# The last four v tiles of a PEER layer, multiplied bank by bank behind the fold of the gathered sums

## Chip, cores and metric

One core of a Trainium2 chip. The metric is the device time of one execution in microseconds; the kernel before took a median of 940.72 us (3 runs, 939.09 to 942.44).

## What is computed

A decoder block for 256 tokens of width 1024. Two attention mixers (MoBA and NSA) and their merge come first; what the change touches is the last part, the PEER expert layer, and the output:

```python
def peer_ffn(h, w_q, sub_k1, sub_k2, expert_u, expert_v):
    ...
    def per_chunk(args):
        xc, ec, gc = args
        u = expert_u[ec]
        a = jnp.einsum('cd,chkd->chk', xc, u).astype(jnp.float32)
        w = (jax.nn.gelu(a) * gc).astype(xc.dtype)
        return jnp.einsum('chk,chkd->cd', w, expert_v[ec])
```

There are 16384 experts (`expert_u` and `expert_v` are 16384 x 1024 float32, 64 MB each). Each token uses 8 heads x 16 experts. The block returns `x + peer_ffn(rmsnorm(x))`.

## The kernel before, in words

The expert layer splits the 256 tokens. For 160 of them (`ND`) the layer is done densely, over all experts: 128 u tiles of 128 experts are loaded (512 KB each) and multiplied with the normed tokens (`u_tile`, L588), Gelu and gate give `ga`, and then 128 v tiles are loaded and multiplied with `ga` (L850 to L858). For the other 96 tokens (`NG`) only the chosen experts' rows are gathered: 96 steps gather 128 u rows each (512 KB) and dot them with the token (L622), 96 steps gather 128 v rows each and add them, weighted, to the sums `accG` on VectorE (L631 and L633).

**The v loop** (L850). For tile `i` eight matmuls, one for each 128 columns of the model width, accumulate over all 128 tiles in four PSUM banks, `acc[0]` to `acc[3]`, two column blocks of 160 tokens each. Then VectorE copies one column of the tile to `mark` (L857), and `gather_steps` issues gather steps, 0.9 a tile (`STEPS_V`), each placed behind the mark on VectorE; from tile 124 on it issues all that are still open. The tiles are loaded on SP's queue (`load_raw`, L580) into nine buffers (three tags of three); tile `i + 9` is loaded when tile `i` has been read by its matmuls and its mark. A gather step (`gathers`, L602) works on rows that POOL fetched by an indirect DMA (L611); there are four row buffers in two pairs, and after every odd step `n` POOL fetches rows `n + 3` and `n + 4`.

**The gathered sums.** `accG` has two sets of 1024 columns (for tokens in groups of 64 and of 32); each set's 128 partitions hold partial sums of several slots of the same token. The steps go through the 64-set and the 32-set of each half of the heads, so the last sixteen steps add to the second set alone. A matmul with the constant matrix `fold` (L865) sums the partials and puts them on the partitions of tokens 0 to 95.

**The end** (L859 to L876). `accT` gets the four banks as copies, two by VectorE, two by ScalarE (L868); its first 96 token columns are cleared on POOL (L860). The result stands as columns by tokens, so it is turned: four PSUM banks `fin`, one for each half of the tokens (`h`) and half of the columns (`j`), take first the folded sums (`h` = 0 only) and then, as matmuls with an identity (L872), the blocks of `accT`. VectorE adds the residual in `x1` (L875), and SP writes 256 KB (L876). This is done four times, one bank after the other.

On each engine the instructions run in a fixed order. It is made when the program is built: in the order of the source, except that work which the builder takes for ready passes work which it takes for late.

Of the kernel before, what the change touches and what calls it, by code (L numbers as in the profile page):

```python
# [18 lines left out]
P = 128  # L19
S = 256  # L20
NH = 2
# [7 lines left out]
NKEY = 128  # L29
# [8 lines left out]
NG = sum(SETS)  # L38
ND = S - NG
STEPS_R = 0.55  # L40
STEPS_U = 0.8
STEPS_V = 0.9
GT = 4
HEAT = 9
AHEAD = 1
# [25 lines left out]
def block_kernel(ctx: ExitStack, tc, x, g2, consts, small, wqkv, wkv5, wmg, w1kv, wup, wout, wq, uT, u, v, folds, out):  # L71
    nc = tc.nc
# [6 lines left out]
    def bank(name, tag, bufs=None):  # L79
        return psum[-1].tile([P, 512], F32, name=name, tag=tag, bufs=bufs)  # L80
# [9 lines left out]
    def C(k):  # L90
        o, n = CONST_OFF[k]
        return cst[:, o:o + n]

    def SM(k):
        o, n = SMALL_OFF[k]
        return sml[:, o:o + n]
# [3 lines left out]
    x1 = hpool.tile([P, NH, DM], F32, name="x1")  # L100
# [43 lines left out]
    with ExitStack() as fs:  # L144
# [49 lines left out]
        for h in range(NH):  # L194
# [3 lines left out]
            for q in range(2):  # L198
# [3 lines left out]
                for c in range(4 * q, 4 * q + 4):  # L202
                    g = SM("g1")[:, c:c + 1]
                    r = slice(h * P, (h + 1) * P)
# [234 lines left out]
        for h in range(NH):  # L439
# [31 lines left out]
            for hh in range(8):  # L471
                j, pair = hh % 2, hh // 2
                nc.tensor.matmul(yb[j * HD:(j + 1) * HD, pair, :], vc[0:N_CMP, hh // 4, :],
                                 pcT[0:N_CMP, hh, :], start=pair == 0, stop=False, skip_group_check=True)
            for pair in range(4):
                g = pair // 2
# [76 lines left out]
    cident = ep.tile([P, P], F32, name="cident")  # L553
    nc.vector.tensor_copy(cident, C("ident"))
    iob = ep.tile([P, P, GT], F16, name="iob")
    nc.vector.tensor_copy(iob, C("iota").unsqueeze(2).to_broadcast([P, P, GT]))
    eTb = ep.tile([P, 2, S], F16, name="eTb")
# [6 lines left out]
    accG = ep.tile([P, len(SETS), DM], F32, name="accG")  # L564
# [6 lines left out]
    def ga_at(i):  # L571
        for b, n, g in ga:
            if b <= i < b + n:
                return g[:, i - b, :]
# [5 lines left out]
    def load_raw(src, i):  # L580
        raw = wp.tile([P, DM], F32, name="uvraw", tag=("wraw", "whi", "wlo")[i % 3])
        nc.sync.dma_start(raw, src[i])
        return raw
# [59 lines left out]
    def gather_steps(rate):  # L643
        gdebt[0] += rate if "rows" in state else 0.0
        while gdebt[0] >= 1 and (state["rows"] == NG or state["steps"] + 6 <= state["rows"]):
            gdebt[0] -= 1
            state["steps"] += 1
            with tc.issue_after(state["dve"].ins):
                next(gather, None)

    with ExitStack() as ts:
# [136 lines left out]
        ahead = []  # L788
# [13 lines left out]
    def gate_group(t0):  # L802
        n = GT
        o2 = op.tile([P, P, n], F16, name="o2")
        o1 = op.tile([P, P, n], F16, name="o1")
        og = [op.tile([P, P, n], F16, name=f"og{i}") for i in range(2)]

        def rows(t):
            return t[:, t0:t0 + n].unsqueeze(1).to_broadcast([P, P, n])

        nc.vector.tensor_tensor(o2, iob, rows(eTb[:, 1]), op=ALU.is_equal)
        nc.vector.tensor_tensor(o1, iob, rows(eTb[:, 0]), op=ALU.is_equal)
        for k in range(n):
            nc.scalar.activation(og[0][:, :, k], o1[:, :, k], AF.Copy, scale=gT[:, t0 + k:t0 + k + 1])  # L814
        nc.vector.tensor_mul(og[1], o1, rows(gTb[:, 1]))
        ps = bank("ps_g", "g").rearrange("p (t i) -> p t i", i=P)
        for k in range(n):
            for i in range(2):
                nc.tensor.matmul(ps[:, k, :], o2[:, :, k], og[i][:, :, k], start=i == 0, stop=i == 1,  # L819
                                 skip_group_check=True)  # L820
        for b, nb, gt in ga:
            g = gt[:, :, t0 - NG:t0 - NG + n]
            src = ps[:, :, b:b + nb].rearrange("p t i -> p i t")
            m = min(max(state["tiles"] - b, 0), nb)
            if m:
                nc.vector.scalar_tensor_tensor(g[:, :m], src[:, :m], 1.0 / GSCALE, g[:, :m], op0=ALU.mult, op1=ALU.mult)
            if m < nb:
                nc.scalar.mul(g[:, m:], src[:, m:], 1.0 / GSCALE)
        state["tokens"] = t0 + n - NG

    groups = ND // GT
    done = 0
    for i in range(TOPK_TILES, NKEY):
        upto = -(-(i + 1 - TOPK_TILES) * groups // (NKEY - TOPK_TILES - GATE_LEAD))
        while done < min(upto, groups):
            gate_group(NG + GT * done)
            done += 1
# [5 lines left out]
    fold = ep.tile([P, len(SETS), P], F32, name="fold")  # L843
    nc.sync.dma_start(fold.rearrange("p k m -> p (k m)"), folds)
    psum_pool(ctx, "ps_f", 1)
    acc = [bank(f"acc{j}", f"acc{j}").rearrange("p (c t) -> p c t", c=2) for j in range(3)]
    acc.append(psd.tile([P, 512], F32, name="acc3", tag="g").rearrange("p (c t) -> p c t", c=2))
    mark = dp.tile([P, 1], F32, name="mark", bufs=1)
    ahead = []
    for i in range(NKEY):  # L850
        while len(ahead) <= AHEAD and i + len(ahead) < NKEY:
            ahead.append(load_raw(v, i + len(ahead)))
        raw = ahead.pop(0)
        for c in range(NC):
            nc.tensor.matmul(acc[c // 2][:, c % 2, 0:ND], raw[:, c * P:(c + 1) * P], ga_at(i),  # L855
                             start=i == 0 and c % 2 == 0, stop=i == NKEY - 1, skip_group_check=True)
        state["dve"] = nc.vector.tensor_copy(mark, raw[:, 0:1])  # L857
        gather_steps(STEPS_V if i < NKEY - 4 else 2 * NG)  # L858
    accT = hpool.tile([P, NC, S], F32, name="accT", tag="h2f")  # L859
    nc.gpsimd.memset(accT[:, :, 0:NG], 0.0)  # L860
    psum.append(psd)
    fin = [[bank("fin", "u", 3) for j in range(2)], [bank("fin", "u", 3), bank("fin1", "g")]]
    for j in range(2):
        for k in range(len(SETS)):
            nc.tensor.matmul(fin[0][j], fold[:, k], accG[:, k, j * 512:(j + 1) * 512], start=k == 0, stop=False,  # L865
                             skip_group_check=True)
    for q in range(4):
        (nc.scalar.copy if q % 2 else nc.vector.tensor_copy)(accT[:, 2 * q:2 * q + 2, NG:], acc[q][:, :, 0:ND])  # L868
    for j in range(2):
        for h in (1, 0):  # L870
            for c in range(4):
                nc.tensor.matmul(fin[h][j][:, c * P:(c + 1) * P], accT[:, 4 * j + c, h * P:(h + 1) * P], cident,  # L872
                                 start=h == 1 and c == 0, stop=c == 3, skip_group_check=True)
            o = x1[:, h, j * 512:(j + 1) * 512]
            nc.vector.tensor_add(o, fin[h][j], o)  # L875
            nc.sync.dma_start(out[h, :, j * 512:(j + 1) * 512], o)  # L876


def topk(nc, sp, vals, idx, src, n):
# [110 lines left out]
```

## Time and profile before

| | us |
|---|---|
| median of 3 runs | 940.72 |
| lowest, highest | 939.09, 942.44 |
| the profiled execution | 938.46 |
| its span, first to last instruction | 936.7 |
| TensorE busy | 900.6 (96%) |
| VectorE busy | 614.3 (66%) |
| ScalarE busy | 309.6 (33%) |
| POOL busy | 218.4 (23%) |
| DMA, all queues | 281.96 MB, mean 301 GB/s |

All times in rows are microseconds from the first instruction of the profiled execution. A busy time of TensorE is modelled, since matmuls are pipelined: 16 instructions that start 0.14 us apart each have a duration of 0.30. "idle before" is how long the engine had stood before an instruction, and what ended that.

### The profile page before, as it was taken

The page shows a single profiled execution, that of the slowest core. Times are in us where ns is not written, and L with a number is a line of the kernel's source. Part 1 is how long each engine was busy: PE and PEld are TensorE (multiplying, and loading weights), DVE is VectorE, ACT ScalarE, POOL GpSimd, SP SyncE. Part 2 cuts the span into 40 slices and gives each one's busy share as a digit, 9 for nine tenths or more (in the row PEclk, how much of TensorE's full clock was granted, in tenths as well). Part 3 has the DMA queues.
Part 4 walks back from the last instruction along what each step waited for, and adds up shares of the span by engine and source line. Part 5 has one row for each costly group of instructions (what it writes and reads, how often), then busy time and mean ns, then how long its engine had stood idle before and what let it go on. Part 6 is the DMA issues. An engine that isn't in the chain of part 4 may idle for free.

```text
span 936.7 us, 17034 instructions
## 1 busy us (share of the span) xinstructions
PE 900.6 (96%) x6433; PEld 842.9 (90%) x6433; DVE 614.3 (66%) x1663; ACT 309.6 (33%) x768; POOL 218.4 (23%) x213
## 2 busy tenths in 40 slices
PE   8999999999999999999999999999989989998987
PEld 6778867998899999999999999999988888988986
DVE  5886876577567689997778788644445544444444
ACT  6766776545541221326555455300000000000000
POOL 2000000000100223233232233333344333443330
PEclk9999999999999999999999999999999999999999
DMA  7665401556556999999999999999999999999994
GB/s 242 191 213 190 159 1 47 183 185 210 169 173 235 331 392 365 376 373 328 350 334 352 354 339 347 354 378 403 357 369 399 400 380 403 385 392 401 400 398 185
DMA packets 79570, 281.96 MB, mean 301 GB/s; under 512 B 10176, under 2 KB 10432, under 8 KB 79488
## 3 DMA queue, kind: packets, MB, share of 16 engines
q1 hardware_dynamic: 51088, 177.63, 52.6%
q0 software_dynamic: 28400, 103.25, 29.2%
q8 instruction: 51, 0.84, 0.3%
q14 instruction: 31, 0.25, 0.1%
HBM read 278.64 MB, written 1.05 MB: 299 GB/s over the span
## 4 chain that ended last, share of the span: by engine, by line
PE 56%; DMA 28%; issue 7%; POOL 3%; DVE 3%; ACT 2%; DVEq 0%; POOLq 0%; ACTq 0%; SPq 0%
PE ps_u L588 28%; DMA grow<-in_v_dram,gidx 21%; PE ps_g L819 4%; POOL grow L611 3%; DMA grow<-in_u_dram,gidx 3%; PE ps_q L121 2%; PE ps_mg L124 2%; PE ps_mg L121 2%; PE ps_q L124 2%; PE ps_q L122 2%; PE ps_mg L122 2%; PE ps_s L410 2%; PE ps_proj L171 1%; PE ps_pt L427 1%; DVE wlo L106 1%
## 5 line engine op out<-in xcount | busy, mean ns | idle before, releaser
L855 PE MATMUL acc<-ga,uvraw 128*128 128x160 f32 x2048 | 292.9, 302 | 21.3 <-DMA uvraw<-in_v_dram 19.5
L855 PEld LDWEIGHTS acc<-ga,uvraw 128*128 128x128 f32 x2048 | 279.9, 190 | 34.2 <-DMA uvraw<-in_v_dram 32.3
L588 PE MATMUL ps_u<-h2f,uvraw 128*128 128x160 f32 x2048 | 287.3, 299 | 0.0
L588 PEld LDWEIGHTS ps_u<-h2f,uvraw 128*128 128x128 f32 x2048 | 280.7, 190 | 0.1
L633 DVE SCALAR_TENSOR_TENSOR accG<-grow,gwt,accG 128x1024 f32<-128x1024 f32 x94 | 120.8, 1285 | 137.0 <-DMA grow<-in_v_dram,gidx 136.9
L611 POOL DMA_INDIRECT grow<-in_u_dram,gidx x96 | 102.1, 1063 | 302.2 <-DVE gdot L622 149.1
L611 POOL DMA_INDIRECT grow<-in_v_dram,gidx x96 | 106.0, 1104 | 166.0 <-DVE mark L857 150.0
L622 DVE CUSTOM_DVE_ANT_0 grow<-grow,h2d 128x1024 f32<-128x1024 f32 x96 | 116.7, 1218 | 34.6 <-DMA grow<-in_u_dram,gidx 34.5
L106 DVE TENSOR_TENSOR wlo<-wraw,whi 128x1024 fp32r<-128x1024 f32 (+1 forms) x80 | 95.5, 1196 | 37.1 <-ACT whi L105 37.0
L105 ACT CAST whi<-wraw 128x1024 fp32r<-128x1024 f32 (+1 forms) x80 | 82.0, 1029 | 65.5 <-PE ps_q L122 13.9
L868 ACT COPY accT<-acc 128x320 f32<-128x320 f32 x2 | 0.9, 426 | 270.9 <-PE acc L855 270.9
L592 ACT ACTIVATE ga<-ps_u 128x160 f32<-128x160 f32 (+32 forms) x124 | 33.5, 271 | 143.7 <-PE ps_u L588 143.4
L814 ACT ACTIVATE og<-o,gT 128x128 f16<-128x128 f16 x160 | 61.9, 568 | 15.9 <-PE ps_g L819 14.5
L819 PE MATMUL ps_g<-og,o 128*128 128x128 f16 x320 | 44.4, 294 | 0.0
L819 PEld LDWEIGHTS <-o 128*128 128x128 f16 x320 | 36.3, 116 | 1.5
L168 PE MATMUL ps_proj<-whi,hhi 128*128 128x512 f32 (+1 forms) x96 | 36.3, 381 | 1.3 <-ACT hhi L205 1.0
L489 POOL DMA_DIRECT2D gain<-in_g_dram x1 | 0.5, 533 | 151.2 <-DVE wlo L106 151.2
L169 PE MATMUL ps_proj<-whi,hlo 128*128 128x512 f32 (+1 forms) x96 | 35.7, 378 | 0.0
L121 PE MATMUL ps_mg<-hhi,whi 128*128 128x256 f32 x128 | 32.3, 288 | 0.0
L596 DVE TENSOR_TENSOR ga<-ga,au 128x160 f32<-128x160 f32 (+32 forms) x68 | 16.8, 247 | 23.4 <-ACT au L595 22.9
L122 PE MATMUL ps_mg<-hlo,whi 128*128 128x256 f32 x128 | 31.9, 285 | 0.0
L121 PE MATMUL ps_q<-h2hi,whi 128*128 128x256 f32 x128 | 31.7, 285 | 0.2 <-ACT h2hi L105 0.2
(256 smaller groups left out, 1126.0 us busy)
## 6 DMA issues: line engine op xcount, KB each, us to landing
uvraw<-in_uT_dram SPq DMA_DIRECT2D x128, 512.0 KB, 6.8
uvraw<-in_v_dram SPq DMA_DIRECT2D x128, 512.0 KB, 7.2
wraw<-in_wqkv_dram SPq DMA_DIRECT2D x20, 512.0 KB, 4.7
wraw<-in_wmg_dram SPq DMA_DIRECT2D x16, 512.0 KB, 3.6
wraw<-in_wq_dram SPq DMA_DIRECT2D x16, 512.0 KB, 4.3
wraw<-in_w1kv_dram SPq DMA_DIRECT2D x8, 512.0 KB, 4.0
wraw<-in_wup_dram SPq DMA_DIRECT2D x8, 512.0 KB, 3.6
wraw<-in_wout_dram SPq DMA_DIRECT2D x8, 512.0 KB, 4.5
```

What stands on the lines that cost most here:

```text
L105: nc.scalar.copy(hi, src)
L106: state["dve"] = nc.vector.tensor_sub(lo, src, hi)
L121: nc.tensor.matmul(ps, lh, rh, start=i == 0, stop=False)
L122: nc.tensor.matmul(ps, ll if lo_last else lh, rh if lo_last else rl, start=False, stop=False)
L124: nc.tensor.matmul(ps, lh if lo_last else ll, rl if lo_last else rh, start=False, stop=i == NC - 1)
L588: state["pe"] = nc.tensor.matmul(ps, raw[:, c * P:(c + 1) * P], h2f[:, c, NG:], start=c == 0, stop=c == NC - 1)
L611: nc.gpsimd.indirect_dma_start(out=dst, out_offset=None, in_=src, in_offset=bass.IndirectOffsetOnAxis(ap=gidx[:, j:j + 1], axis=0))
L622: nc.vector.tensor_tensor_reduce(out=g, in0=g, in1=h2d[k], scale=1.0, scalar=0.0, op0=ALU.mult, op1=ALU.add, accum_out=gdot[:, j:j + 1])
L633: nc.vector.scalar_tensor_tensor(accG[:, k], g, gwt[:, j:j + 1], accG[:, k], op0=ALU.mult, op1=ALU.add)
L814: nc.scalar.activation(og[0][:, :, k], o1[:, :, k], AF.Copy, scale=gT[:, t0 + k:t0 + k + 1])
L819: nc.tensor.matmul(ps[:, k, :], o2[:, :, k], og[i][:, :, k], start=i == 0, stop=i == 1, skip_group_check=True)
L855: nc.tensor.matmul(acc[c // 2][:, c % 2, 0:ND], raw[:, c * P:(c + 1) * P], ga_at(i), start=i == 0 and c % 2 == 0, stop=i == NKEY - 1, skip ...
```

## The change

The v loop stops at tile 123; from tile 120 on (124 before) it issues all gather steps that are still open. Then the last four tiles are loaded into `raws` as before, and the folded sums are put into `fin`. The four `fin` banks are cut otherwise: each holds both halves of the tokens for 256 columns, so bank `q` of `fin` needs bank `q` of `acc` alone. Then, for each bank `q`, the matmuls of all four tiles for its two column blocks finish `acc[q]`, `accT` gets its copy, and the bank before (`q - 1`) is turned, added and written out (`finish`). Outputs go to SP's queue for banks 0 and 2, to ACT's for 1 and 3. The last four tiles have no mark.

```diff
+LAST = 4
...
-    for i in range(NKEY):
+
+    def v_load(i):
         while len(ahead) <= AHEAD and i + len(ahead) < NKEY:
             ahead.append(load_raw(v, i + len(ahead)))
-        raw = ahead.pop(0)
+        return ahead.pop(0)
+
+    for i in range(NKEY - LAST):
+        raw = v_load(i)
         for c in range(NC):
             nc.tensor.matmul(acc[c // 2][:, c % 2, 0:ND], raw[:, c * P:(c + 1) * P], ga_at(i),
-                             start=i == 0 and c % 2 == 0, stop=i == NKEY - 1, skip_group_check=True)
+                             start=i == 0 and c % 2 == 0, stop=False, skip_group_check=True)
         state["dve"] = nc.vector.tensor_copy(mark, raw[:, 0:1])
-        gather_steps(STEPS_V if i < NKEY - 4 else 2 * NG)
+        gather_steps(STEPS_V if i < NKEY - 2 * LAST else 2 * NG)
     accT = hpool.tile([P, NC, S], F32, name="accT", tag="h2f")
     nc.gpsimd.memset(accT[:, :, 0:NG], 0.0)
     psum.append(psd)
-    fin = [[bank("fin", "u", 3) for j in range(2)], [bank("fin", "u", 3), bank("fin1", "g")]]
-    for j in range(2):
+    raws = [v_load(i) for i in range(NKEY - LAST, NKEY)]
+    outr = out.rearrange("h p d -> p h d")
+    fin = [bank("fin", "u", 3).rearrange("p (h d) -> p h d", h=NH) for _ in range(3)]
+    fin.append(bank("fin3", "g").rearrange("p (h d) -> p h d", h=NH))
+    for q in range(4):
         for k in range(len(SETS)):
-            nc.tensor.matmul(fin[0][j], fold[:, k], accG[:, k, j * 512:(j + 1) * 512], start=k == 0, stop=False,
+            nc.tensor.matmul(fin[q][:, 0], fold[:, k], accG[:, k, q * 256:(q + 1) * 256], start=k == 0, stop=False,
                              skip_group_check=True)
+
+    def finish(q):
+        for h in range(NH):
+            for c in range(2):
+                nc.tensor.matmul(fin[q][:, h, c * P:(c + 1) * P], accT[:, 2 * q + c, h * P:(h + 1) * P], cident,
+                                 start=False, stop=c == 1, skip_group_check=True)
+        r = slice(q * 256, (q + 1) * 256)
+        nc.vector.tensor_add(x1[:, :, r], fin[q], x1[:, :, r])
+        (nc.scalar if q % 2 else nc.sync).dma_start(outr[:, :, r], x1[:, :, r])
+
     for q in range(4):
+        for c in (2 * q, 2 * q + 1):
+            for i in range(LAST):
+                nc.tensor.matmul(acc[q][:, c % 2, 0:ND], raws[i][:, c * P:(c + 1) * P], ga_at(NKEY - LAST + i),
+                                 start=False, stop=i == LAST - 1, skip_group_check=True)
         (nc.scalar.copy if q % 2 else nc.vector.tensor_copy)(accT[:, 2 * q:2 * q + 2, NG:], acc[q][:, :, 0:ND])
-    for j in range(2):
-        for h in (1, 0):
-            for c in range(4):
-                nc.tensor.matmul(fin[h][j][:, c * P:(c + 1) * P], accT[:, 4 * j + c, h * P:(h + 1) * P], cident,
-                                 start=h == 1 and c == 0, stop=c == 3, skip_group_check=True)
-            o = x1[:, h, j * 512:(j + 1) * 512]
-            nc.vector.tensor_add(o, fin[h][j], o)
-            nc.sync.dma_start(out[h, :, j * 512:(j + 1) * 512], o)
+        if q:
+            finish(q - 1)
+    finish(3)
```

## Rows read from the trace of the kernel before

**Rows 1.** The page: TensorE's busy time; GB/s in 40 slices of the span.

```profile
PE 900.6 (96%) x6433; PEld 842.9 (90%) x6433; DVE 614.3 (66%) x1663; ACT 309.6 (33%) x768; POOL 218.4 (23%) x213
...
GB/s 242 191 213 190 159 1 47 183 185 210 169 173 235 331 392 365 376 373 328 350 334 352 354 339 347 354 378 403 357 369 399 400 380 403 385 392 401 400 398 185
```

**Rows 2.** Table by stage: stretch, length, busy us (instructions), clock, DMA share, GB/s.

```profile
850.00:900.00 50.00, 46.00 (x320) 43.79 (x320) 24.59 (x38) 0.00 (x0) 21.29 (x18) 1.00 1.01 399
...
921.00:937.00 16.00, 11.05 (x69) 8.73 (x67) 6.70 (x16) 0.85 (x2) 0.00 (x0) 0.93 0.21 78
```

**Rows 3.** Chain of waits, 880 to 937 us: start, us, what.

```profile
916.68 0.15 DVE mark L857
...
916.89 6.03 DMA uvraw<-in_v_dram
922.91 0.14 issue
923.05 2.41 PE acc L855 x16
925.46 3.43 PE fin L865 x8
928.89 3.59 PE fin L872 x32
```

**Rows 4.** Timeline, 900 to 937 us: start, us, engine, line, count, idle before.

```profile
901.15 16.39 PE L855 MATMUL acc<-ga,uvraw 128*128 128x160 f32 x112 [1.54 <-DMA uvraw<-in_v_dram]
...
915.50 0.93 POOL L611 DMA_INDIRECT grow<-in_v_dram,gidx  x1 [0.30 <-issue]
...
918.05 4.58 PE L855 MATMUL acc<-ga,uvraw 128*128 128x160 f32 x32 [0.50 <-DMA uvraw<-in_v_dram]
...
921.72 0.33 DVE L857 COPY mark<-uvraw 128x1 f32<-128x1 f32 x2
922.62 1.28 DVE L633 SCALAR_TENSOR_TENSOR accG<-grow,gwt,accG 128x1024 f32<-128x1024 f32 x1 [0.57 <-DMA grow<-in_v_dram,gidx]
...
923.82 0.52 DVE L857 COPY mark<-uvraw 128x1 f32<-128x1 f32 x3
...
924.62 0.53 DVE L857 COPY mark<-uvraw 128x1 f32<-128x1 f32 x3 [0.28 <-DVE mark L857]
...
928.73 3.73 PE L872 MATMUL fin<-cident,accT 128*128 128x128 f32 x32
```

**Rows 5.** Line 860: durations ns, first and last start us.

```profile
L860 POOL MEMSET accT<- x1: 743/743/743, 615.0 to 615.0; 128x768 f32 x1
```

**Rows 6.** Timeline of TensorE, 380 to 470 us.

```profile
392.70 30.59 PE L588 MATMUL ps_u<-h2f,uvraw 128*128 128x160 f32 x224
...
426.28 0.45 PE L588 MATMUL ps_u<-h2f,uvraw 128*128 128x160 f32 x2
```

**Rows 7.** Timeline of TensorE, 0 to 9.5 us.

```profile
1.24 3.59 PE L192 MATMUL ps_heat<-heat 128*128 128x512 bf16 x8 [1.24 <-DVE heat L189]
4.63 1.90 PE L201 MATMUL pt_row<-cst,x 128*128 128x128 f32 x8
...
6.93 0.30 PE L169 MATMUL ps_proj<-whi,hlo 128*128 128x280 f32 x1
7.06 0.30 PE L168 MATMUL ps_proj<-whi,hhi 128*128 128x280 f32 x1
8.23 1.10 PE L201 MATMUL pt_row<-cst,x 128*128 128x128 f32 x8 [0.87 <-DMA x<-in_x_dram]
```

**Rows 8.** Table by stage, the end: columns as in rows 2.

```profile
934.50:936.70 2.20, 0.00 (x0) 0.00 (x0) 0.00 (x0) 0.00 (x0) 0.00 (x0) 0.57 0.12 44
```

**Rows 9.** Groups of instructions by shape, 916 to 937 us: busy us, mean ns.

```profile
L875 DVE TENSOR_TENSOR x<-fin,x 128x512 f32<-128x512 f32 x4 | 2.8, 691 | 4.5 <-PE fin L872 4.5
...
L868 ACT COPY accT<-acc 128x320 f32<-128x320 f32 x2 | 0.9, 426 | 270.9 <-PE acc L855 270.9
```

**Rows 10.** DMA issues, 900 to 937 us: count, KB each, median us to landing.

```profile
out_dram<-x SPq DMA_DIRECT2D x4, 256.0 KB, 2.0
```

## The prediction

> **What bounds the kernel now.** I read the page first. TensorE is busy 96% of the span, and the last ten slices of forty move about 400 GB/s [rows 1]. So two things are nearly full at once, and the average doesn't say which one ends the work. The table by stage does: in 850 to 900 us the DMA share is 1.01 while TensorE, at full granted clock, lacks work for 4 of 50 us; after 921 the DMA share is 0.21 [rows 2]. The v stage therefore ends when the transfers end, and behind it stands a tail that is TensorE's alone. The chain of waits shows the hand-over: the mark of tile 118 frees the slot of tile 127, nine tiles on; that load lands at 922.91; tile 127 is multiplied (2.41), the gathered sums are folded (3.43), the sums are turned (3.59) [rows 3]. Tail after the last landing: 923.05 to 932.46 (last row of [rows 4]), then the last add and an output DMA.
>
> Who is where in the tail must be counted. A v tile is 16 TensorE instructions (8 matmuls, each two passes). The row of 16 at 923.05 is tile 127, the 32 at 918.05 are tiles 125 and 126, the 112 that end at 917.54 are tiles 118 to 124. So tile 124 runs in the last 2.2 to 2.4 us of that row, and tile 123 ends at about 915.3 [rows 3, 4]. On VectorE, six marks stand behind the last gather step (122 to 127), two just before it (120 and 121); the last step runs from 922.62 to 923.90 and had waited for its row from DRAM [rows 4]. At 0.9 steps a tile every tenth tile has none; here that is tile 120.
>
> **The change, part by part.**
>
> Earlier flush: all steps still open are issued from tile 120 instead of 124. By the count one step is open then, the last, and it moves from behind mark 121 to behind mark 120. Its row was asked for at 915.50 [rows 4], behind the step four before it, which doesn't move, and the step waits for the landing. Gain: 0. The loads of tiles 124 to 127 wait for marks 115 to 118, which stay; the four marks that go (124 to 127, 0.15 us each) have nothing behind them that is late. So the last v tile lands at 922.91 as before and the last step ends at 923.90 as before.
>
> The fold goes ahead of the last four tiles. What stands behind a late instruction on its engine waits with it: the marks of tiles 122 to 126 run after the last step, though these tiles had long landed [rows 4]. So the place counts. The order is fixed when the program is built and lets ready work pass work that is late: the clearing of accT, written behind all v tiles, runs at 615.0 [rows 5], and a u tile's 16 instructions are broken after two by gate matmuls [rows 6]. But in the v stage marks and steps alternate exactly as written, so the builder took rows as timely, and I put the fold where the source has it: behind tile 123. There TensorE arrives at 915.3 and finds the sums ready at 923.90. It stands 8.7 us; before, it used that time for tiles 124 to 126.
>
> Restart: 923.90 plus 0.14 (landing to matmul at 922.91 [rows 3]) is 924.05. From there on everything is TensorE's and all data are there:
> - fold: 16 matmul passes of 256 columns in place of 8 of 512, the same columns, 3.43 us [rows 3]. By the piece the bounds are 16 passes at the pitch of 160 columns (30.59 / 224 = 0.137, 2.2 us [rows 6]) and at that of 512 (3.43 / 8 = 0.43, 6.9 us); I take the same columns, since the pitches of the two sizes stand to each other nearly as the columns do.
> - four tiles: 64 passes of 0.137 = 8.74 us. Bank order changes neither number nor size.
> - turning: 32 passes as before, 3.59 us [rows 3].
>
> Sum 15.76, end 939.81 at full clock, against 932.46: **+7.35 us**. A piece may come off: the first pair of passes of the fold reads the half of the sums that is complete sixteen steps sooner, and could run at 915.3 (-0.43). Not shown; I take 0.
>
> The clock. TensorE starts the program with 128x512 passes 0.43 us apart and eight 128x128 turns in 1.90 us; from 8.23 on eight of these take 1.10 [rows 7]. So it ran at 1.2 GHz, the lower of its two levels, from its first matmul at 1.24 to 6.53 at least, and at 2.4 GHz at 6.93, where matmuls of 280 columns start 0.13 apart, which at the pace of the 512 would be 0.23. At the end the granted clock falls inside 934.5 to 936.7 (mean 0.57, so about 934.8), 2.3 us after the last matmul [rows 8]. A stop of 8.7 us is almost four times that. I expect the clock down at 924.05 and up again after as long as at the start, 5.3 to 5.7 us, say 5.4; half of it is lost: **+2.7 us**. Bounds: 0, if it stays up, and 5.4, if the return takes twice as long.
>
> The Trainium skill says the same of gaps in the middle of a kernel ("TensorE: Matmul & The Clock Gate", section on HAM oscillation): a wait for a DMA between bursts throttles the engine and the next burst starts at half rate. No run here shows such a gap; by that rule the sum is +10.05, without it +7.35.
>
> Copies, adds, outputs: each copy of a bank (0.43 us on ScalarE [rows 9]) runs under the next bank's 2.19 us, the last under the 0.9 us in which bank 2 is turned; if that cover went, 0.4 us would show. Four adds of the same 128x512 elements stay; three run under TensorE as now. Outputs go alternately to SP and ACT. An ACT issue waits for its add, and the copy of bank 3 is queued behind it; it has 2.2 us for that add (0.69 [rows 9]) and issue. The last output is again 256 KB, 2.0 us to landing from SP [rows 10]. ACT issues none now, so the difference isn't shown: no gain, since the last issue has nothing queued ahead of it on SP either, up to the 0.93 of a gather's issue on POOL [rows 4]; I take SP's price, so 0.
>
> Total: +7.35 + 2.7 = **+10.05 us**. The profiled execution took 938.46, 2.26 under the median of 940.72; the sum gives 948.5 from its own time and 950.8 from the median, which I give.
>
> **The rivals.**
> - The clock stays up or returns at once: +7.35, 948.1. For it: no stop in the middle shows a fall. Against: it fell 2.3 us after the end.
> - The change doesn't do what it says: the built order lets the banks pass the late fold. Then TensorE waits for tile 127 with three matmuls of the other tiles done; 58 of 64 passes remain (7.92), from 923.05 to 930.97, then fold and turning: 937.99, +5.5, 946.2. For it: the two places where work has passed other work [rows 5, 6]. Against: the regular alternation of marks and steps.
> - The last row lands by 915, and the fold is free. The banks still need tile 127: 930.97 + 3.59 = 934.56, +2.1, 942.8: within what can be told apart. The bank order itself costs that: it leaves nearly four tiles behind the last landing, where now one is left. Against: the row landed at about 922.6, asked for at 915.50, on full DMA.
> - Not slower: row and tile 127 both land before the fold is through at 918.7, so TensorE never stops: 915.3 + 15.76 = 931.1, -1.4, 939.3. It decides once the last transfers end 4.2 us sooner. At the 400 GB/s of [rows 1] that is 1.7 MB, three tiles, that would have to go elsewhere; no byte is removed.
>
> **How the numbers follow.** Chances: forecast 0.64, clock stays up 0.14, fold passed by 0.10, row early 0.07, no stop 0.05. A measurement tells 0.3% (2.8 us) from no change. Slower by more: the first three, 0.88. Same: the row-early case and about half of the last, 0.09; faster 0.03, since even there the gain is under 0.3% and only scatter carries it over. Range: low end the stop without loss of clock, less the 0.43, on the profiled time, 938.46 + 6.9 = 945.4; high end the clock's upper bound on the median, 940.72 + 7.35 + 5.4 = 953.5. It takes in the first three cases.
>
> **What would show it.** In the new profile: TensorE idle some 8 to 9 us behind tile 123, ended by the last gather step; the last load landing near 923 as before; then fold, 64 passes and 32 turns without a gap; a granted clock of 0.5 in the first 3 to 6 us of them; last add near 942.5 instead of 932.5. Wrong if the fold stands behind the banks, if the idle time is under 4 us, or if the last landing moves by more than 2 us.

## The result and the profile after

The changed kernel took 955.0 us (median; 951.28 to 956.9) where the kernel before took 941.58 (939.09 to 945.92) on the same chip: ratio 1.0123, 95% interval 1.0085 to 1.016, so 11.6 us slower, between 8.0 and 15.1. (Differences in us, here and below, are the ratio times the median of the kernel before beside it; these two medians lie 13.4 apart.) Two runs of e4, one of e11 and one of the kernel before beside a2 (954.49 us) fell into a slower state of the chip and are left out of every difference and range below. A second set of runs of the same kernel (below, a2) gave 9.0, between 5.8 and 12.0. The forecast was 10.05 slower. The 955.0 itself lies 1.5 over the high end of the stated range; the 952.17 of the second set lies inside it.

The profiled execution took 954.38 us, its span 952.6. Its page, TensorE's busy time and the GB/s of 40 slices, answers to [rows 1]:

```profile
PE 904.8 (95%) x6441; PEld 846.4 (89%) x6441; DVE 614.3 (64%) x1659; ACT 310.2 (33%) x768; POOL 224.1 (24%) x213
...
GB/s 240 190 217 181 151 1 68 181 186 208 163 186 246 363 338 397 346 390 335 352 346 357 332 345 349 347 389 358 376 383 398 401 398 394 377 388 395 370 351 45
```

TensorE is busy 4.2 us longer although it does the same products. The last slice (24 us) moves 45 GB/s where it was 185: TensorE works longer with hardly a transfer beside it. The end of the chain of waits answers to [rows 3] (start, us, what):

```profile
928.65 0.06 DVE accG L634
...
929.85 0.16 DVE mark L862
930.01 6.06 PE fin L873 x14
936.07 4.35 PE acc L888 x32
940.42 0.89 PE fin L879 x8
941.31 2.18 PE acc L888 x16
943.48 0.89 PE fin L879 x8
944.37 2.18 PE acc L888 x16
946.55 1.80 PE fin L879 x16
948.35 0.02 issue
948.37 0.69 DVE x L882
```

The releaser at the end is no longer the landing of tile 127 but the last gather step, and behind it stands TensorE without a gap: the fold (L873), the four tiles in bank order (L888) with the turning (L879) between. The timeline of the same stretch, with the idle time before each row in brackets, answers to [rows 4]:

```profile
918.69 2.44 PE L860 MATMUL acc<-ga,uvraw 128*128 128x160 f32 x16 [0.47 <-DMA uvraw<-in_v_dram]
...
920.97 0.59 PE L873 MATMUL fin<-accG,fold 128*128 128x256 f32 x2
...
928.65 1.28 DVE L634 SCALAR_TENSOR_TENSOR accG<-grow,gwt,accG 128x1024 f32<-128x1024 f32 x1 [0.98 <-DMA grow<-in_v_dram,gidx]
...
929.99 6.08 PE L873 MATMUL fin<-accG,fold 128*128 128x256 f32 x14 [8.42 <-DVE mark L862]
...
949.10 0.38 ACTq L883 DMA_DIRECT2D out_dram<-x  x1
```

The row of 16 at 918.69 is tile 123. Behind it two passes of the fold run at once, and then TensorE stands 8.42 us until the step of 928.65 to 929.93 is done. The table by stage answers to [rows 2] (stretch, length, busy us of PE, PEld, DVE, ACT, POOL, then the granted clock, DMA share, GB/s):

```profile
850.00:900.00 50.00, 44.86 (x313) 42.48 (x312) 23.24 (x36) 0.00 (x0) 17.32 (x18) 1.00 1.01 391
...
925.00:930.00 5.00, 0.01 (x1) 0.01 (x1) 2.70 (x4) 0.00 (x0) 0.00 (x0) 0.54 0.51 202
930.00:935.00 5.00, 5.00 (x12) 4.01 (x13) 0.31 (x2) 0.00 (x0) 0.00 (x0) 0.50 0.01 3
935.00:940.00 5.00, 5.00 (x35) 4.80 (x34) 0.49 (x1) 0.00 (x0) 0.00 (x0) 0.93 0.00 0
```

The granted clock falls during the stop (0.54 on average in 925 to 930, so from about 925.4 on), is 0.50 for the first five microseconds of the restart, and returns soon after 935: twelve passes in 930 to 935, thirty-five in the next five.

From here on "the tail" is the time from the end of the last gather step to the end of TensorE's last row. Before: 923.90 to 932.46 [rows 4], 8.56 us. After: 929.93 to 948.34, 18.41 us. The two profiled executions differ by 15.92 us: **9.85 of them in the tail**, and 6.03 ahead of it, by which the last step ended later. Up to the end of the last step the order on VectorE and POOL is the same in both kernels, but for mark 121, which now stands behind the last step; a2 shows what that lateness is.

### The profile page after: what moved, and what is told of

It is laid out like the page before. It is cut to its first block, busy times and chain, and to the rows that moved or that the text cites. A ratio compares the mean times of both kernels' runs of the same rounds, so it can differ in the third digit from the quotient of the medians.

```text
span 952.6 us, 17039 instructions
## 1 busy us (share of the span) xinstructions
PE 904.8 (95%) x6441; PEld 846.4 (89%) x6441; DVE 614.3 (64%) x1659; ACT 310.2 (33%) x768; POOL 224.1 (24%) x213
## 4 chain that ended last, share of the span: by engine, by line
PE 55%; DMA 30%; issue 5%; DVE 5%; POOL 2%; ACT 2%; SPq 0%; POOLq 0%; DVEq 0%; ACTq 0%
PE ps_u L589 25%; DMA grow<-in_v_dram,gidx 21%; DMA grow<-in_u_dram,gidx 4%; PE ps_g L820 4%; POOL grow L612 2%; PE ps_q L122 2%; PE ps_mg L125 2%; PE ps_mg L122 2%; PE ps_q L125 2%; PE ps_q L123 2%; PE ps_mg L123 2%; PE ps_s L411 2%; PE ps_proj L172 1%; PE ps_proj L170 1%; PE ps_proj L169 1%
## 5 line engine op out<-in xcount | busy, mean ns | idle before, releaser
L860 PE MATMUL acc<-ga,uvraw 128*128 128x160 f32 x1984 | 284.8, 302 | 24.0 <-DMA uvraw<-in_v_dram 22.3
L860 PEld LDWEIGHTS acc<-ga,uvraw 128*128 128x128 f32 x1984 | 271.1, 190 | 37.5 <-DMA uvraw<-in_v_dram 34.6
L612 POOL DMA_INDIRECT grow<-in_u_dram,gidx x96 | 108.2, 1127 | 301.1 <-DVE gdot L623 147.7
```

The source lines that it names most:

```text
L612: nc.gpsimd.indirect_dma_start(out=dst, out_offset=None, in_=src, in_offset=bass.IndirectOffsetOnAxis(ap=gidx[:, j:j + 1], axis=0))
```

## The experiments

The theory: the fold, put ahead of the last four tiles, makes TensorE wait for the last gather step; the work that covered this wait now runs behind it, the first microseconds at half clock. The rivals: the bank order and what comes with it (small passes, copies, outputs from two queues) is slow by itself; or the clock has no part. The earlier flush (all open steps from tile 120 on) is in a2, e1 to e5 and e9; in e5 it goes with no loss that can be told from nothing.

**a2: the changed kernel once more, with no edit.**

> The changed kernel once more, unedited, beside the others. From the two profiles its tail, from the end of the last gather step to TensorE's end, is 9.9 us longer than before's: 10 us over the kernel before, whatever the v stage ahead of it takes in a single run.

Ratio 1.0095 (1.0062 to 1.0127), +9.0 us. In its profiled execution (948.8 us), the timeline of TensorE and VectorE:

```profile
915.34 0.59 PE L873 MATMUL fin<-accG,fold 128*128 128x256 f32 x2
...
923.70 1.28 DVE L634 SCALAR_TENSOR_TENSOR accG<-grow,gwt,accG 128x1024 f32<-128x1024 f32 x1 [0.96 <-DMA grow<-in_v_dram,gidx]
...
925.04 5.40 PE L873 MATMUL fin<-accG,fold 128*128 128x256 f32 x14 [9.11 <-DVE mark L862]
...
940.76 1.95 PE L879 MATMUL fin<-cident,accT 128*128 128x128 f32 x16
```

Here TensorE arrives at the fold at 915.34, where the prediction had 915.3, and ends at 942.71; the prediction's 939.81 plus 2.7 is 942.5. That the two ends meet is luck: the last step ended 1.1 us later than predicted, and the early pair of the fold (0.43) and a cheaper return of the clock (2.2 in place of 2.7) take nearly as much off. The same program thus arrives 5.6 us earlier than in the first profile (920.97): a lateness of this size is scatter of the v stage from one execution to the next. The kernel before scatters as well: its 30 runs beside this set took 938.25 to 950.15.

**e2: the fold ahead of the last four tiles in the kernel before, everything else but the earlier flush as it was** (four tiles in their own order, 512-column passes, outputs on SP).

```
+        if i == NKEY - 4:
+            accT = ...; fin = ...
+            for j in range(2):
+                for k in range(len(SETS)):
+                    nc.tensor.matmul(fin[0][j], fold[:, k], accG[:, k, j * 512:(j + 1) * 512], ...)
...
-        gather_steps(STEPS_V if i < NKEY - 4 else 2 * NG)
+        gather_steps(STEPS_V if i < NKEY - 8 else 2 * NG)
```

> The kernel before with one edit: the fold ahead of the last four tiles, which stay tile by tile, their end as it was. Theory: TensorE stands 8 to 9 us behind tile 123 and restarts at half clock: 9 to 10 us over the kernel before, as much as the whole change. Rival (the bank order costs it): within 2 us of the kernel before.

Ratio 1.0103 (1.0072 to 1.0134), +9.7 us. Its timeline of TensorE:

```profile
914.67 1.02 PE L861 MATMUL fin<-accG,fold 128*128 128x512 f32 x2
923.83 5.49 PE L861 MATMUL fin<-accG,fold 128*128 128x512 f32 x6 [8.13 <-DVE mark L866]
929.11 9.01 PE L864 MATMUL acc<-ga,uvraw 128*128 128x160 f32 x64
```

and the table by stage, with the clock as the third number from the end:

```profile
919.20:929.30 10.10, 5.47 (x7) 2.37 (x8) 3.62 (x10) 0.00 (x0) 0.00 (x0) 0.50 0.24 96
```

The early fold gives a loss as large as the whole change's without the bank order, with the same stop (8.13) and the same fall of the clock. The tail is 923.77 to 941.69, 17.92. The rival that puts the loss on the bank order alone falls.

**e1: the bank order without the early fold.** In the changed kernel the fold's four passes of a bank move into `finish(q)`, right ahead of the bank's turning.

```
-    for q in range(4):
+    def finish(q):
         for k in range(len(SETS)):
             nc.tensor.matmul(fin[q][:, 0], fold[:, k], accG[:, k, q * 256:(q + 1) * 256], ...)
-
-    def finish(q):
```

> The changed kernel with the fold taken from ahead of the last four tiles and put, four passes at a time, ahead of each bank's turning. Theory (TensorE stood behind the fold, for the last gather step, and lost clock): it now waits for tile 127 alone, and 58 of 64 passes, fold and turning lie behind that landing: 5 to 6 us over the kernel before, with no stop longer than 4 us and the clock full. Rival (the bank order itself costs it, wherever the fold stands): about 10 us over the kernel before, as the change.

Ratio 1.0076 (1.0041 to 1.0111), +7.2 us; 1.2 over what was expected at most. The interval (3.9 to 10.5) holds the expected 5 to 6 and the rival's 10 alike, so the time doesn't decide; the profile does, since the stop of 8 us behind tile 123 is gone. What the expectation missed is the clock. The timeline of TensorE:

```profile
925.07 0.43 PE L886 MATMUL acc<-ga,uvraw 128*128 128x160 f32 x2
927.20 0.51 PE L886 MATMUL acc<-ga,uvraw 128*128 128x160 f32 x2 [1.69 <-DMA uvraw<-in_v_dram]
930.07 0.87 PE L886 MATMUL acc<-ga,uvraw 128*128 128x160 f32 x2 [2.35 <-DMA uvraw<-in_v_dram]
933.02 5.33 PE L886 MATMUL acc<-ga,uvraw 128*128 128x160 f32 x26 [2.08 <-DMA uvraw<-in_v_dram]
```

The table by stage:

```profile
925.00:929.30 4.30, 1.02 (x6) 0.56 (x4) 2.22 (x3) 0.00 (x0) 0.76 (x1) 1.00 1.02 406
929.40:936.20 6.80, 4.06 (x14) 3.72 (x15) 3.52 (x9) 0.00 (x0) 0.00 (x0) 0.50 0.25 96
```

With the bank order TensorE can do two passes per landed tile and then waits for the next: 1.69, 2.35, 2.08 us. The bank order does cost by itself, because it leaves 58 of 64 passes behind the landing of tile 127, as the prediction's second and third rivals counted. The expectation had the clock full, since no single wait is long; it was 0.50 from 929.4, within the second of these waits, to 936.2. The 26 passes took 5.33 us where 26 at 0.137 are 3.56, so about 1.8 us of the 7.2 are the clock; 5.5 plus 1.8 is 7.3. Taking the early fold back therefore saves little: early fold alone 9.7, bank order alone 7.2, both together 9.0 (a2). They don't add, since either leaves most of the four tiles' work behind a transfer that lands late.

**e3 and e9: the stop filled with work that nobody needs.** Eight and eleven extra 512-column matmuls (16 and 22 passes) behind tile 123 and ahead of the fold.

```
+    with tc.issue_after(last.ins):
+        for i in range(8):      # e9: 11
+            nc.tensor.matmul(fin[3].rearrange("p h d -> p (h d)"), cident, x1[:, 0, 0:512], start=True, stop=True, ...)
```

> The changed kernel with eight matmuls of 512 columns, whose result is overwritten, between tile 123 and the fold (some 6.9 us of the stop). Theory: the clock stays at 1.00 and the fold takes 3.0 in place of 6.1 us: 2.8 us less than the change, that is 7 us over the kernel before. Rival (the clock's loss is not on the path): as the change, 10 us over.

e3: ratio 1.0069 (1.0035 to 1.0103), +6.5 us. Its profiled execution doesn't fit the reason, though, as the timeline shows:

```profile
920.02 7.03 PE L873 MATMUL fin<-x,cident 128*128 128x512 f32 x16
...
929.59 4.98 PE L877 MATMUL fin<-accG,fold 128*128 128x256 f32 x14 [2.11 <-DVE mark L862]
```

and the table by stage:

```profile
930.00:933.00 3.00, 3.00 (x9) 2.38 (x8) 0.00 (x0) 0.00 (x0) 0.00 (x0) 0.50 0.01 3
```

A remaining wait of 2.11 us was enough: the clock fell as the fold began, and the tail (929.53 to 946.83, 17.3) is only 1.1 us shorter. So the clock's part was not settled by this run, and the fill was made longer.

> The changed kernel with eleven 512-column matmuls (22 passes of 0.43 us, 9.6 us) between tile 123 and the fold; with eight of them the wait left over was 2.11 us and the clock still fell. My theory has two separate terms, the wait and the low clock behind it. By it the fill covers the wait; if no idle time above 1 us is left, the granted clock stays at 1.0 to the end of TensorE's work, the fold's passes run 0.21 us apart, and from the end of the last gather step to TensorE's end it takes 15.5 us plus what the fill overruns (0 to 1), in place of 18.4 in the changed kernel: 6 to 8 us over the kernel before. The rival, that the clock falls near the end whatever TensorE does, has it at 0.5 within the fold again, and the tail at 17.5 us or more.

The timeline of TensorE and VectorE in e9:

```profile
917.20 9.60 PE L873 MATMUL fin<-x,cident 128*128 128x512 f32 x22
...
925.34 1.29 DVE L634 SCALAR_TENSOR_TENSOR accG<-grow,gwt,accG 128x1024 f32<-128x1024 f32 x1 [1.15 <-DMA grow<-in_v_dram,gidx]
...
926.64 3.62 PE L877 MATMUL fin<-accG,fold 128*128 128x256 f32 x16
```

and its table by stage:

```profile
926.60:930.00 3.40, 3.40 (x17) 2.97 (x16) 0.39 (x4) 0.00 (x0) 0.00 (x0) 1.00 0.01 2
```

Now the last step ended at 926.63, just as the fill ended; TensorE never stood, the clock stayed at 1.00, and all 16 passes of the fold took 3.62 us where 14 of them took 6.08. The tail is 926.63 to 942.52, 15.89: 2.5 us shorter than in the changed kernel with two passes (0.43) more in it, so the low clock costs about 2.9. The rival without the clock falls. The time, 1.0091 (1.0055 to 1.0127), +8.6 us, lies 0.6 over what was expected at most, and its interval (5.2 to 12.0) can't show 2.5 us beside a2's 9.0; what the clock costs is read from the profiles alone.

**e4: the rows sooner.** 1.0 gather steps a v tile in place of 0.9 (`STEPS_V = 1.0`) in the changed kernel, to have the sums complete when TensorE comes.

> The changed kernel with 1.0 gather steps a tile in place of 0.9, so that the last step stands behind mark 108 and the sums are ready before tile 123. Theory: no stop at the fold; what is left is the bank order's price, up to 58 passes and the turning behind the last landing: 0 to 3 us over the kernel before. Rival (the stop is not due to the late rows): about 10 us over.

A miss: 966.32 and 967.05 us, 23 over the 943.71 beside it. From the timelines of TensorE and VectorE:

```profile
924.57 1.28 DVE L634 SCALAR_TENSOR_TENSOR accG<-grow,gwt,accG 128x1024 f32<-128x1024 f32 x1
...
945.11 3.62 PE L873 MATMUL fin<-accG,fold 128*128 128x256 f32 x16
```

The stop is gone: the fold runs right behind tile 123, at full clock. But the rows didn't come sooner (last step at 924.57; before, 922.62), while tile 123 ended at 945.1 in place of 915.3. With more steps among the marks, the marks stand behind steps that wait for rows, and the v loads wait for the marks: fifteen marks, of tiles 109 to 123, still stand behind the last step, where before only the last six tiles' marks did. By these two profiles the rows keep their pace and hold the v tiles to it; no run tests that by itself.

**e5: the same change for one tile in place of four** (`LAST = 1`, all open steps still issued from tile 120).

> The changed kernel with one tile, not four, behind the fold and in bank order. Theory (what is lost is TensorE's stop ahead of tiles that could have been multiplied meanwhile): tiles 124 to 126 now fill the wait for the last step, the stop is under 2.5 us, the clock stays, and behind the step lie fold, 16 passes and turning in place of 16 passes, fold and turning: 0 to 1.5 us over the kernel before. Rival (bank order or the second output queue costs time of its own): 3 us or more over.

```profile
928.23 3.29 PE L873 MATMUL fin<-accG,fold 128*128 128x256 f32 x14 [1.50 <-DVE accG L634]
```

Ratio 1.0004 (0.9979 to 1.0030), +0.4 us. The stop shrinks to 1.50 us, the 14 passes take 3.29 at full clock, the tail is 9.19. With one tile behind the fold in place of four the loss is gone, and the bank order, the second output queue and the earlier flush are all still there.

**e8: only the half of the fold whose sums are complete sixteen steps sooner is put ahead of the last four tiles**, in the kernel before; the other half stays behind them.

```
+        if i == NKEY - 4:
+            for j in range(2):
+                nc.tensor.matmul(fin[0][j], fold[:, 0], accG[:, 0, j * 512:(j + 1) * 512], start=True, stop=False, ...)
...
-        for k in range(len(SETS)):
-            nc.tensor.matmul(fin[0][j], fold[:, k], accG[:, k, ...], start=k == 0, stop=False, ...)
+        nc.tensor.matmul(fin[0][j], fold[:, 1], accG[:, 1, ...], start=False, stop=False, ...)
```

> The kernel before with only the half of the fold whose sums are complete sixteen steps earlier put ahead of the last four tiles. Theory (an early fold costs only if its sums are late): no stop behind tile 123, and 1.7 us of the tail go: 1 to 2 us under the kernel before. Rival (any fold ahead of the tiles makes the stop): 9 to 10 us over.

```profile
919.33 1.88 PE L860 MATMUL fin<-accG,fold 128*128 128x512 f32 x4
921.05 9.60 PE L863 MATMUL acc<-ga,uvraw 128*128 128x160 f32 x64
930.48 1.88 PE L868 MATMUL fin<-accG,fold 128*128 128x512 f32 x4
```

Ratio 0.9989 (0.9960 to 1.0018), -1.0 us, which the interval can't tell from nothing. There is no stop: it isn't folding early that costs, but folding early what isn't there yet.

**e6, e10, e11: the other way round.** If the last row is what comes last, everything that doesn't need it should run ahead of it. e6 turns the v tiles' sums first (all four copies on ScalarE, the h = 1 half added and written out at once) and folds last, and issues 0.87 steps a tile; e10 has only the rate, e11 only the order.

```
-STEPS_V = 0.9
+STEPS_V = 0.87                                         # e6, e10
...
-        gather_steps(STEPS_V if i < NKEY - 4 else 2 * NG)
+        gather_steps(STEPS_V if i < NKEY - 1 else 2 * NG)  # this and the rest: e6, e11
...
+    for h in (1, 0):
+        for j in range(2):
+            for c in range(4):
+                turn = nc.tensor.matmul(fin[h][j][:, c * P:(c + 1) * P], accT[...], cident, ...)
+            if h == 1: ...
+    with tc.issue_after(turn.ins):
+        for k in range(len(SETS)):
+            for j in range(2):
+                nc.tensor.matmul(fin[0][j], fold[:, k], accG[:, k, j * 512:(j + 1) * 512], ...)
```

> The opposite order: the kernel before with 0.87 gather steps a tile, so that v tiles come in ahead of the last rows; all banks copied by ScalarE and turned first, and the fold behind everything. If the rows' own pace sets the end (last step ending near 924, as in every profile so far in which nothing else was late), only the fold and the adds are left behind it: PE path 3.4 in place of 8.6 us, 3 to 6 us under the kernel before. If the last landing moves later by as much as the tiles come earlier, within 2 us of the kernel before.

e6: ratio 0.9947 (0.9922 to 0.9973), -5.0 us (the medians lie 4.0 apart), faster than both kernels. The end of its timeline:

```profile
915.56 9.03 PE L855 MATMUL acc<-ga,uvraw 128*128 128x160 f32 x64 [1.03 <-DMA uvraw<-in_v_dram]
...
924.43 3.73 PE L868 MATMUL fin<-cident,accT 128*128 128x128 f32 x32
...
930.87 1.28 DVE L633 SCALAR_TENSOR_TENSOR accG<-grow,gwt,accG 128x1024 f32<-128x1024 f32 x1 [0.93 <-DMA grow<-in_v_dram,gidx]
...
932.21 3.67 PE L877 MATMUL fin<-accG,fold 128*128 128x512 f32 x4 [2.33 <-DVE mark L857]
```

Tiles and turning are through at 928.16, and behind the last step only four passes are left: a tail of 3.73 us in place of 8.56. Those four run at about half the clock (3.67 us, where the same four took 1.88 in e8). The gain itself stands in the medians, not in this profile: the execution took 941.88, one of the slowest of its twelve, its last step ended 8.25 us later than before's (932.15), and TensorE ended later too (935.88; 932.46). So the expected time came, but the reason given for it, a last step near 924, is not what the profile shows.

> The kernel before with 0.87 gather steps a tile in place of 0.9 and nothing else. The version with the fold last (5.0 us under) changed the rate and the order of the tail at once. If the order gave that, the rate alone gives nothing or costs: about four steps more stand open at tile 124 and delay the fold, 0 to 4 us over the kernel before. If the rate gave it (v loads held up less), this is 3 to 5 us under.

> The version with the fold last, with 0.9 gather steps a tile as in the kernel before: the order of the tail alone. If the order gave the 5 us, this is 3 to 6 us under the kernel before: TensorE turns the sums of the v tiles while the last gather steps run, and only the fold's second half, an add and an output stand behind the last step. If the rate gave it, this is within 1.5 us of the kernel before.

e10: 0.9973 (0.9949 to 0.9998), -2.5 us; e11: 0.9982 (0.9949 to 1.0015), -1.7 us. By these figures neither gives the 5.0 alone, so both expectations, that one of the two gives it all, are missed; but both intervals reach down to 4.8 under, so that either gives nearly all of it is not ruled out. In e10 the early end of the v tiles is partly lost again, because the fold then waits for the rows and runs at half clock:

```profile
927.78 5.49 PE L865 MATMUL fin<-accG,fold 128*128 128x512 f32 x6 [5.30 <-DVE mark L857]
```

In e11 TensorE is not through with the tiles before the rows are, and turns and folds without a wait:

```profile
927.68 3.73 PE L868 MATMUL fin<-cident,accT 128*128 128x128 f32 x32
931.25 3.60 PE L877 MATMUL fin<-accG,fold 128*128 128x512 f32 x8
```

A lower rate ends the tiles sooner and the rows later; the order makes later rows cheap. That the two need each other fits both profiles, but it isn't shown: 2.5 and 1.7 may merely add.

## Why the prediction was right

**What ends last.** The prediction read from [rows 2 to 4] that the end waits for transfers and that the tail is TensorE's alone. So it was: the tail of the changed kernel runs with the DMA share at 0.01 or less up to 940. With the change the last transfer that counts is a gathered row in place of tile 127.

**The place of the fold.** It was argued from the regular order of marks and steps that the built order would not let the banks pass the late fold. The chain shows the fold right behind the last step, the banks behind it. The rival "passed by" falls, and so do "row early" and "no stop" with the wait of 8.42 us (8.7 predicted; 9.11 in a2, where the step ended 1.1 us later than before).

**The early pair.** It ran ahead of the stop (920.97, 915.34), the piece that the prediction named and took as 0: 0.43 us too much.

**The pieces at full clock.** Fold: 16 passes in 3.62 us (e9), so the columns count and not the passes, as taken. Four tiles: 4.35 + 2.18 + 2.18 = 8.71 in the chain (8.74). Turning: 0.89 + 0.89 + 1.80 = 3.58 (3.59). No copy, add or issue stands in the chain between them: the costs of zero were right. From the last add's end (949.06) to the end of the span it is 3.5 us, as before (the last add follows TensorE's end at 932.46 and takes 0.69 [rows 4, 9]; the span was 936.7): an output from ACT costs no more there than one from SP.

**The clock.** Predicted 2.7 us from the clock's return at the start of the program; about 2.9 by e9, and 3.0 by the 14 passes themselves (6.06 against 14 x 0.215 = 3.0); 2.2 in a2, where the 14 take 5.40 in place of 6.08, and 2.7 in e2 (six passes from 923.83 to 929.11, which at 0.43 each are 2.6). That the clock would be down was right; the size is in part luck. It was read from the pace of the first instructions in a single execution, where the table by stage gives a granted clock of 1.00 for all of 0 to 8 us, so nothing but that pace speaks for a low clock there. And the pace itself changes: the eight turns that took 1.90 us at 4.63 [rows 7] took 1.04 in a2:

```profile
4.49 1.04 PE L202 MATMUL pt_row<-cst,x 128*128 128x128 f32 x8
```

By the same reading the return there came within 3.3 us of the first matmul, and the term would have been 1.6 at most. The granted clock is 0.50 in 930 to 935, behind a stop that ended with a row's landing and its step. The sentence of the Trainium skill ("TensorE: Matmul & The Clock Gate", section on HAM oscillation), that a wait for a DMA throttles the engine and the next burst starts at half rate, agrees with that.

**The sum.** 10.05 less 0.43 for the early pair, plus 0.2 for the clock, is 9.82; measured are 9.85 us in the first profile, 9.2 in a2 (924.98 to 942.71, less 8.56). What the forecast left out is the v stage's scatter of some 6 us from one execution to the next. By its own test (a last landing moved by more than 2 us) the first profile would have spoken against it; only a2, with the step 1.1 us from where it was before, showed that this was scatter. The range was made of the tail's bounds alone, and 955.0 lay above it. Whether the change also moves the mean of the v stage by a microsecond or two, the intervals leave open.

## What to carry to other kernels

Work that needs the operand that comes last belongs last. Ask of a move not how much it removes but what it stood behind before and what stands behind it now: here about 7.2 of the 8.74 us of multiplying (all but the end of tile 127, 923.90 to 925.46) had covered the wait for the last row for nothing. Where a late operand can't come sooner, put all that doesn't need it ahead of it and keep behind it the least that does (e6), and split an operation whose one half is ready early (e8).

## What the hardware showed that was not expected

- The granted clock can fall on much less than a long stop: two waits of 1.69 and 2.35 us with two passes between them (e1), or one of 2.11 us behind 7 us of dense passes (e3), brought it to 0.50 for 3 to 7 us. A wait of 1.50 us in e5 didn't; its 14 passes took 3.29. But the length of the wait doesn't decide: a wait of 3.28 us in e4, which ended at 765.08, left the clock at 1.00 (760 to 775). And all thirteen profiles have the same wait of 2.0 us for ScalarE, which ends between 239.2 and 242.1 us; by 246 us the clock has fallen to 0.50 in six (e1, e4, e5, e6, e10, e11) and has stayed at 1.00 in seven. The table by stage of the kernel before and of e5:

```profile
242.00:244.00 2.00, 2.00 (x20) 2.00 (x18) 0.94 (x3) 1.14 (x2) 0.00 (x0) 1.00 0.20 45
...
242.00:244.00 2.00, 2.00 (x10) 1.76 (x10) 1.63 (x4) 1.49 (x4) 0.00 (x0) 0.50 0.46 109
```

- A fall can come after work has begun again: in e3 TensorE restarted at 929.59 and the clock is 0.98 on average up to 930, then 0.50.
- The gathered rows keep their own pace: with 1.0 in place of 0.9 steps asked for per v tile (e4) the last step came 2 us later, not sooner. The v loads, held back through the marks, ended some 19 us later (about 942, by a DMA share of 0.99 in 939 to 941, 0.31 in 941 to 943 and 0 behind; before, 922.91), and tile 123 was multiplied some 30 us later.
